# Row sums of reciprocals: a new division of the squaring and summing over four engines, and no batch statistics

## The chip, the cores and the metric

The kernel runs on one NeuronCore of a Trainium2 chip. Its engines are TensorE (PE), VectorE (DVE), ScalarE (ACT), GpSimd (POOL) and SyncE (SP), each with an instruction stream of its own; they meet only at semaphores. SP issues all transfers here, and 16 DMA engines carry them out in the order of issue. The metric is the device time of one execution in microseconds (us), lower being better. A profiled execution has its own time and a span, which goes from the first to the last profiled instruction of the program.

## The reference

```python
x = np.abs(np.random.randn(32, 512, 1024)).astype(np.float32) + 1e-6

def reference(x):
    return np.sum(1.0 / x, axis=-1).astype(np.float32)
```

The input has 67.1 MB and is read once; the output has 64 KB. The kernel divides nowhere: ScalarE computes 1/sqrt(x), and the square of that is 1/x. Each row of 1024 numbers needs three steps then: reciprocal root, square, sum.

## The kernel before

The 16384 rows of x are laid over 128 partitions, 128 rows to each, so that "row u" below is a tile of 128 x 1024 numbers (0.52 MB), one row in every partition. Row 127 is split into two pieces, numbered 127 and 128, of 640 and 384 columns (`PIECES`). The rows go through `ring`, which has 46 places: row u lies at place u modulo 46, so row u can only be loaded when everything that reads row u-46 is done. Results go to `sums`, one column a row.

The order of the work is written out by hand in `PLAN`, a list of tokens. Each engine takes its tokens in this order; a token such as `A35+3` names the operation, the first row and the number of rows, `U59@0` an operation and a buffer. The program adds a semaphore wait wherever a token needs what another engine wrote or still reads. The operations:

- D: a load of so many rows (line 163), always the next ones. SP issues in order, so a load that waits for a place holds up those behind it. There are eight semaphores for the transfers, taken in turn: a transfer also waits until the eighth one before it has landed.
- A: reciprocal root on ScalarE in place (line 170, "Arsqrt"). C: square on ScalarE in place (line 170). Z: square on ScalarE with the sum as a by-product (line 178), followed by a read of the accumulator.
- G: square on GpSimd in place (line 244). T: sum on VectorE (line 247), which follows a C or a G.
- Q: square and sum in one pass on VectorE (line 224), with both inputs the same row of the ring, followed by a read of the accumulator.
- B: two batch-statistics operations on VectorE, one for each half row (line 238). They give count, mean and variance for the even and the odd elements, from which the sum of squares is worked out later. K (lines 258 to 269) does that on GpSimd for rows 0 to 63 and again for rows 64 to 115, five small operations each; M (line 276) adds the outcome to `sums`.
- U, P, L, E, R: another way for 7 of the rows. With a and b the halves of a row, 1/a + 1/b = (a + b)/(ab). TensorE adds the halves into PSUM by products with the identity matrix (U, line 191), GpSimd multiplies them (P, line 184), ScalarE takes reciprocal root and square of the half row ab (L and E, line 201), VectorE multiplies the two and sums (R, line 210).
- O: the early stores of `sums[:, 0:116]`, six of them (line 154); the last twelve columns are stored at the end.

The plan opens with loads of 2, 9, 10, 12 and 13 rows, which fill the ring. Towards the end the loads get short, down to one row, and nearly every row is an A on ScalarE followed by a Q on VectorE. The last tokens are `A117+2 Q116 M0 O0 A119+2 Q117 Q118 A121 Q119 Z120 Q121 A122 A123 Q122 A124 Q123 A125 Q124 A126 Q125 A127 A128 Q127 Z126 Q128`.

Of the kernel before, what the change touches and what calls it, by code (L numbers as in the profile page):

```python
# [11 lines left out]
def kernel(  # L12
# [5 lines left out]
    nc = tc.nc  # L18
    f32 = mybir.dt.float32
    P = 128  # L20
    D = 1024
    H = D // 2
    F = 128
    R = 46
    NP = 5
    PIECES = (640, 384)
    NR = F - sum(PIECES) // D
    KB = (0, 64, 116)
    S = float(2**17)
    FIT = 1.0 - 2.0**-17  # L30

# [2 lines left out]

    PLAN = """
        D2 D9 D10 D12 D13 A0+2 C0 Z1 T0 A2+6 A8 G2 A9 A10 G3+2 T2 C5 C7+2 T5 G6 T8 T3 A11 G9
        A12+3 T4 T6+2 G10 A15 T9 A16+3 A19+2 B17 G18 C11 C12 C13 T10+3 D11 C14 C16 Z15 T13+2 A21  # L40
        A22+5 T16 A27 G19+4 A28+5 Z23 Z24 G25+2 T18+5 D11 Z27 Z31 Z32 G28+3 A33 A34 T25+2 A35+3
        B33 A38+5 G35+3 T28 T29+2 D10 A43+3 Q39 G40 Z34 T35+2 Z38 G42 A46 T37 D7 A47+3 T40 G43
        B41 T42 A50+4 G46 T43 G48 B45 T46 A54 G50 A55+2 B47 T48 G52 Z44 D7 T50 Z49 G56 B51 Z54
        T52 D7 U59@0 A57+2 P59@0 Q53 P60@1 L59 A61+3 B55 U60@1 T56 D4 B57 L60 A64 B58 D4 A65 B61
        A66+2 B62 D2 E59 G66 E60 B64 Z63 R59 K0+64 Z65 D3 R60 T66 U75@2 A68+2 B67 A70 B68 D3
        P75@2 A71 Q69 A72 G71 B70 D2 A73+2 L75 B73 A76+2 T71 A78+2 B74 G76 B77 A80 G79 T76 A81
        B78 A82 A83 T79 A84 B80 E75 Z72 D2 D2 D1 D2 D1 D1 D1 B81 D1 D1 A85 R75 Q82 A86+3 B83 Q85
        A89+3 Q86 B87 Z84 G91 B88 Z89 B90 A92+2 P95@3 U95@3 T91 A94 Q92 L95 Q93 A96 A97 Q94 G96
        U102@4 A98 B97 A99+3 B98 P102@4 T96 L102 B99 G100 E95 U103@5 A104+3 R95 B101 P103@0 T100
        P108@1 L103 A107 B105 U108@6 G106 L108 B107 E102 E103 R102 E108 K64+52 R103 A109+3 T106  # L50
        R108 Z104 Q109 A112 Q110 A113+2 Q111 Q112 A115+2 Q113 Z114 Q115 A117+2 Q116 M0 O0 A119+2
        Q117 Q118 A121 Q119 Z120 Q121 A122 A123 Q122 A124 Q123 A125 Q124 A126 Q125 A127 A128
        Q127 Z126 Q128
    """.split()

    Arsqrt = mybir.ActivationFunctionType.Abs_reciprocal_sqrt
# [19 lines left out]
        tc.tile_pool(name="pspool", bufs=1, space=bass.MemoryType.PSUM)  # L76
    )
    ring = pool.tile([P, R, D], f32)
    stats = pool.tile([P, F, 2, 2, 3], f32)
    part = pool.tile([P, F, 4], f32)  # L80
    total_b = pool.tile([P, F], f32)
    sums = pool.tile([P, F], f32)
    prod = pool.tile([P, NP, H], f32)
    ident = pool.tile([P, P], f32)
    ps = pspool.tile([P, 8, H], f32)
    make_identity(nc, ident)
    nc.gpsimd.memset(stats, 0.0)  # L87
    nc.gpsimd.memset(sums, 0.0)

    def parse(tok):  # L90
        body, _, b = tok[1:].partition("@")
# [3 lines left out]
    def place(u):  # L95
        if u < NR:
            return u, 0, D
        at = sum(PIECES[: u - NR])
        return NR + at // D, at % D, PIECES[u - NR]

    def area(u, n=1):
        r, at, w = place(u)
        return ring[:, r % R : r % R + n, at : at + w]
# [52 lines left out]
    with tc.manual_schedule():  # L156
        for op, u, n, b in (parse(tok) for tok in PLAN):
# [11 lines left out]
            elif op in "AC":  # L169
                inst = nc.scalar.activation(  # L170
                    out=area(u, n),
                    in_=area(u, n),
                    func=Arsqrt if op == "A" else Square,
                    scale=FIT if op == "A" else 1.0,
                )
                note("ACT", inst, writes=rows(u, n))
            elif op == "Z":
                inst = nc.scalar.activation(  # L178
                    out=area(u), in_=area(u), func=Square, accum_out=sums[:, u : u + 1]
                )  # L180
                note("ACT", inst, writes=rows(u))
            elif op == "P":
                slot[u], r = b, u % R
                inst = nc.gpsimd.tensor_tensor(  # L184
                    out=prod[:, b], in0=ring[:, r, :H], in1=ring[:, r, H:], op=mult
                )
                note("POOL", inst, rows(u), [("slot", b)])
            elif op == "U":
                bank[u], r = b, u % R
                for h in range(2):  # L190
                    inst = nc.tensor.matmul(  # L191
                        ps[:, b],
                        lhsT=ident,
                        rhs=ring[:, r, h * H : (h + 1) * H],
                        start=h == 0,
                        stop=h == 1,
                    )
                    note("PE", inst, half(u, h * H), [("bank", b)])
            elif op in "LE":
                pair = prod[:, slot[u]]  # L200
                inst = nc.scalar.activation(  # L201
                    out=pair,
                    in_=pair,
                    func=Arsqrt if op == "L" else Square,
                    scale=S * FIT if op == "L" else 1.0,
                )
                note("ACT", inst, writes=[("slot", slot[u])])
            elif op == "R":
                pair = prod[:, slot[u]]
                inst = nc.vector.tensor_tensor_reduce(  # L210
                    out=pair,
                    in0=pair,
                    in1=ps[:, bank[u]],
                    scale=S,
                    scalar=0.0,
                    op0=mult,
                    op1=add,
                    accum_out=sums[:, u : u + 1],
                )
                note("DVE", inst, [("bank", bank[u])], [("slot", slot[u])])  # L220
            elif op == "Q":
                row, r = area(u), place(u)[0]
                total = sums[:, r : r + 1]
                inst = nc.vector.tensor_tensor_reduce(  # L224
                    out=row,
                    in0=row,
                    in1=row,
                    scale=1.0,
                    scalar=total if r in summed else 0.0,
                    op0=mult,  # L230
                    op1=add,
                    accum_out=total,
                )
                summed.add(r)
                note("DVE", inst, writes=rows(u))
            elif op == "B":
                for h in range(2):
                    inst = nc.vector.bn_stats(  # L238
                        out=stats[:, u, h], in_=ring[:, u % R, h * H : (h + 1) * H]
                    )  # L240
                    note("DVE", inst, reads=half(u, h * H))
            elif op == "G":
                row = area(u, n)
                inst = nc.gpsimd.tensor_tensor(out=row, in0=row, in1=row, op=mult)  # L244
                note("POOL", inst, writes=rows(u, n))
            elif op == "T":
                inst = nc.vector.tensor_reduce(  # L247
                    out=sums[:, u : u + n],
                    in_=area(u, n),
                    axis=mybir.AxisListType.X,  # L250
                    op=add,
                )
                note("DVE", inst, reads=rows(u, n))
            elif op == "K":
                mean = stats[:, u : u + n, :, :, 1].rearrange("p f h e -> p (f h e)")
                var = stats[:, u : u + n, :, :, 2].rearrange("p f h e -> p (f h e)")
                flat = part[:, u : u + n].rearrange("p f q -> p (f q)")
                nc.gpsimd.tensor_tensor(out=flat, in0=mean, in1=mean, op=mult)  # L258
                nc.gpsimd.tensor_scalar(  # L259
                    out=flat, in0=flat, scalar1=float(H // 2), scalar2=None, op0=mult  # L260
                )
                nc.gpsimd.tensor_tensor(out=flat, in0=flat, in1=var, op=add)  # L262
                nc.gpsimd.tensor_tensor(  # L263
                    out=part[:, u : u + n, :2],
                    in0=part[:, u : u + n, :2],
                    in1=part[:, u : u + n, 2:],
                    op=add,
                )
                nc.gpsimd.tensor_tensor(  # L269
                    out=total_b[:, u : u + n],  # L270
                    in0=part[:, u : u + n, 0],
                    in1=part[:, u : u + n, 1],
                    op=add,
                )
            elif op == "M":
                nc.gpsimd.tensor_tensor(  # L276
                    out=sums[:, : KB[-1]],
                    in0=sums[:, : KB[-1]],
                    in1=total_b[:, : KB[-1]],
                    op=add,  # L280
                )
            elif op == "O":
                for c in range(0, KB[-1], 20):
                    store(c, min(c + 20, KB[-1]))
        store(KB[-1], F)


# [28 lines left out]
```

## Time and profile before

| | |
|---|---|
| median of 3 runs | 167.15 us (166.9 to 167.3) |
| the profiled execution's own time | 166.88 us |
| its span | 165.0 us |
| busy: ACT, DVE, POOL, PE | 149.0, 122.1, 85.2, 20.5 us |
| load queue, share of 16 DMA engines' span | 95.9% |
| read from HBM | 67.11 MB, 407 GB/s over the span |

The page of the profile gives the busy time of each engine, the DMA queues, the chain of waits that ended last and the costliest groups of instructions. "Lnnn" is a line of the kernel. A group's line gives the tiles, the shape, the count, the busy time in us and the mean duration in ns, and then the idle time of the engine ahead of it and what ended that. A line of the timeline gives start and duration in us, engine, line, operation, tiles and shapes, and the number of merged instructions. A table by stretches gives, for each stretch, the busy time of PE, PEld, DVE, ACT and POOL with their instruction counts, the granted clock of TensorE, the busy share of the DMA engines and GB/s; a share counts whole packets where they end or begin and can so pass 1. In the lines on DMA issues stand the size in KB and the time from issue to landing, and SPq is the issuing queue.

### The profile page before, as it was taken

The page shows a single profiled execution, that of the slowest core. Times are in us where ns is not written, and L with a number is a line of the kernel's source. Part 1 is how long each engine was busy: PE and PEld are TensorE (multiplying, and loading weights), DVE is VectorE, ACT ScalarE, POOL GpSimd, SP SyncE. Part 2 cuts the span into 40 slices and gives each one's busy share as a digit, 9 for nine tenths or more (in the row PEclk, how much of TensorE's full clock was granted, in tenths as well). Part 3 has the DMA queues.
Part 4 walks back from the last instruction along what each step waited for, and adds up shares of the span by engine and source line. Part 5 has one row for each costly group of instructions (what it writes and reads, how often), then busy time and mean ns, then how long its engine had stood idle before and what let it go on. Part 6 is the DMA issues. An engine that isn't in the chain of part 4 may idle for free.

```text
span 165.0 us, 529 instructions
## 1 busy us (share of the span) xinstructions
PE 20.5 (12%) x28; PEld 7.0 (4%) x28; DVE 122.1 (74%) x161; ACT 149.0 (90%) x131; POOL 85.2 (52%) x52
## 2 busy tenths in 40 slices
PE   0000000000000000000019026000009764000000
PEld 0000000000000000000013011000002211000000
DVE  0020027954920499999999999899998999999992
ACT  3630997999999999999999999999999999999992
POOL 5000069922019999999996088380043889403000
PEclk9999999999999999999999965555555589955555
DMA  5999989899999998989998999999999999999960
GB/s 183 500 429 445 447 367 489 381 500 453 413 413 413 413 524 349 513 362 470 404 453 367 467 381 440 445 438 417 424 408 429 433 414 426 423 423 421 404 204 2
DMA packets 4754, 67.19 MB, mean 407 GB/s; under 512 B 1424, under 2 KB 1552, under 8 KB 2192
## 3 DMA queue, kind: packets, MB, share of 16 engines
q1 hardware_dynamic: 4752, 67.18, 95.9%
q14 instruction: 2, 0.02, 0.0%
HBM read 67.11 MB, written 0.07 MB: 407 GB/s over the span
## 4 chain that ended last, share of the span: by engine, by line
ACT 43%; DMA 39%; DVE 14%; issue 1%; SPq 1%; DVEq 0%
DMA ring<-in_x_dram 39%; ACT ring L170 35%; DVE sums L247 7%; ACT ring L178 6%; DVE ring L224 4%; DVE stats L238 3%; ACT prod L201 3%; SPq L163 1%; DVE sums L224 0%; DVEq L224 0%; DVEq L311 0%
## 5 line engine op out<-in xcount | busy, mean ns | idle before, releaser
L170 ACT ACTIVATE ring<-ring 128x1024 f32<-128x1024 f32 (+4 forms) x74 | 120.0, 1688 | 12.1 <-DMA ring<-in_x_dram 12.0
L244 POOL TENSOR_TENSOR ring<-ring 128x1024 f32<-128x1024 f32 (+3 forms) x26 | 66.5, 2581 | 56.7 <-ACT ring L170 56.7
L247 DVE TENSOR_REDUCE sums<-ring 128x1 f32<-128x1024 f32 (+3 forms) x33 | 50.6, 1563 | 35.9 <-POOL ring L244 23.4
L238 DVE BATCH_NORM_STATS2 stats<-ring 128x6 f32<-128x512 f32 x62 | 38.7, 677 | 2.5 <-ACT ring L170 2.5
L191 PE MATMUL ps<-ring,ident 128*128 128x512 f32 x28 | 20.5, 878 | 117.8 <-POOL ring L244 86.0
L224 DVE CUSTOM_DVE_ANT_0 ring<-ring 128x1024 f32<-128x1024 f32 (+1 forms) x25 | 30.8, 1281 | 1.5 <-ACT ring L170 1.3
L178 ACT ACTIVATE ring<-ring 128x1024 f32<-128x1024 f32 x21 | 21.8, 1040 | 0.0
L191 PEld LDWEIGHTS ps<-ring,ident 128*128 128x128 f32 x28 | 7.0, 272 | 130.4 <-POOL ring L244 86.0
L184 POOL TENSOR_TENSOR prod<-ring 128x512 f32<-128x512 f32 x7 | 9.9, 1420 | 0.6 <-DMA ring<-in_x_dram 0.5
L201 ACT ACTIVATE prod<-prod 128x512 f32<-128x512 f32 x14 | 8.1, 615 | 0.0
L276 POOL TENSOR_TENSOR sums<-sums,total_b 128x116 f32<-128x116 f32 x1 | 1.3, 1256 | 7.4 <-DVE sums L224 7.4
L210 DVE CUSTOM_DVE_ANT_0 prod<-prod,ps 128x512 f32<-128x512 f32 x7 | 4.6, 674 | 0.0
L178 ACT ACTIVATION_READ_ACCUMULATOR ring<-ring 128x1 f32 x21 | 3.9, 187 | 0.0
L224 DVE DVE_READ_ACCUMULATOR2_ANT sums<- 128x1 f32 x26 | 2.1, 82 | 0.0
L65 ACT ACT_TABLE_LOAD x1 | 1.3, 1283 | 0.7 <-PEq L300 0.7
L259 POOL TENSOR_SCALAR part<-part 128x256 f32<-128x256 f32 (+1 forms) x2 | 1.6, 792 | 0.2
L262 POOL TENSOR_TENSOR part<-part,stats 128x256 f32<-128x256 f32 (+1 forms) x2 | 1.5, 748 | 0.2
L87 POOL MEMSET stats<- 128x1536 f32 x1 | 1.4, 1378 | 0.0
L258 POOL TENSOR_TENSOR part<-stats 128x256 f32<-128x256 f32 (+1 forms) x2 | 1.2, 596 | 0.0
L263 POOL TENSOR_TENSOR part<-part 128x128 f32<-128x128 f32 (+1 forms) x2 | 0.8, 381 | 0.2
L224 DVE CUSTOM_DVE_ANT_0 ring<-ring,sums 128x384 f32<-128x384 f32 x1 | 0.6, 618 | 0.1
L269 POOL TENSOR_TENSOR total_b<-part 128x64 f32<-128x64 f32 (+1 forms) x2 | 0.6, 296 | 0.2
(8 smaller groups left out, 1.7 us busy)
## 6 DMA issues: line engine op xcount, KB each, us to landing
ring<-in_x_dram SPq DMA_DIRECT2D x2, 5632.0 KB, 26.7
ring<-in_x_dram SPq DMA_DIRECT2D x3, 3584.0 KB, 32.4
ring<-in_x_dram SPq DMA_DIRECT2D x2, 5120.0 KB, 28.4
ring<-in_x_dram SPq DMA_DIRECT2D x1, 6656.0 KB, 56.1
ring<-in_x_dram SPq DMA_DIRECT2D x6, 1024.0 KB, 30.1
ring<-in_x_dram SPq DMA_DIRECT2D x1, 6144.0 KB, 41.1
ring<-in_x_dram SPq DMA_DIRECT2D x1, 4608.0 KB, 15.4
ring<-in_x_dram SPq DMA_DIRECT2D x2, 2048.0 KB, 39.4
```

The source lines that it names most:

```text
L163: inst = nc.sync.dma_start(out=area(u, m), in_=x_v[:, r : r + m, at : at + w])
L170: inst = nc.scalar.activation(out=area(u, n), in_=area(u, n), func=Arsqrt if op == "A" else Square, scale=FIT if op == "A" else 1.0,)
L178: inst = nc.scalar.activation(out=area(u), in_=area(u), func=Square, accum_out=sums[:, u : u + 1])
L184: inst = nc.gpsimd.tensor_tensor(out=prod[:, b], in0=ring[:, r, :H], in1=ring[:, r, H:], op=mult)
L191: inst = nc.tensor.matmul(ps[:, b], lhsT=ident, rhs=ring[:, r, h * H : (h + 1) * H], start=h == 0, stop=h == 1,)
L201: inst = nc.scalar.activation(out=pair, in_=pair, func=Arsqrt if op == "L" else Square, scale=S * FIT if op == "L" else 1.0,)
L210: inst = nc.vector.tensor_tensor_reduce(out=pair, in0=pair, in1=ps[:, bank[u]], scale=S, scalar=0.0, op0=mult, op1=add, accum_out=sums[:, ...
L224: inst = nc.vector.tensor_tensor_reduce(out=row, in0=row, in1=row, scale=1.0, scalar=total if r in summed else 0.0, op0=mult, op1=add, acc ...
L238: inst = nc.vector.bn_stats(out=stats[:, u, h], in_=ring[:, u % R, h * H : (h + 1) * H])
L244: inst = nc.gpsimd.tensor_tensor(out=row, in0=row, in1=row, op=mult)
L247: inst = nc.vector.tensor_reduce(out=sums[:, u : u + n], in_=area(u, n), axis=mybir.AxisListType.X, op=add,)
L259: nc.gpsimd.tensor_scalar(out=flat, in0=flat, scalar1=float(H // 2), scalar2=None, op0=mult)
```

## The change

The plan is rewritten, and B, K and M leave it, with the tiles `stats`, `part` and `total_b` and two memsets on GpSimd. By token, before and after:

| token | before: tokens (rows) | after: tokens (rows) |
|---|---|---|
| D | 26 | 28 |
| A | 66 (122) | 74 (124) |
| C | 8 (9) | 5 (5) |
| Z | 21 | 24 |
| G | 26 (35) | 29 (35) |
| T | 33 (44) | 24 (39) |
| Q | 26 | 60 |
| B | 31 | 0 |
| V | 0 | 1 |
| U, P, L, E, R | 7 each | 5 each |
| early stores | 6 | 3 |

Counts of A and Q include the two pieces of row 127. V is new: a VectorE operation that multiplies one row by 1, adds 0 and sums on the way. It stands in place of a T for row 2, which GpSimd squared. The pieces of row 127 have 512 columns each. The plan opens with loads of 2, 9, 9, 10, 6 and 10 rows. The rows of U, P, L, E, R are 28, 71, 92, 101 and 105.

```diff
-    PIECES = (640, 384)
+    PIECES = (512, 512)
     NR = F - sum(PIECES) // D
-    KB = (0, 64, 116)
+    DONE = 116
+    PART = 39
...
     PLAN = """
...
+        D2 D9 D9 D10 D6 D10 A0 A1 Q0 Z1 A2+5 A7+3 G2 G4+3 V2 A10 Z3 Z7 Z8 A11 G9 T4 A12+2 T5 G10
+        A14 T6 D7 A15 G12 T9+2 A16+2 G13 A18+2 Q15 Z14 G18 Z17 T13 Z19 Q16 C11 P28@0 U28@0 A20+2
+        T11+2 D9 A22+4 G20+2 T18 A26 Q23 G24 A27 T20+2 L28 A29 G25 A30+2 A32 G26 A33+3 G29 Z32
+        G30+2 T29 Z33 E28 C22 R28 C27 T22 G34 T24+4 D9 A36+2 G35 A38+2 G36+2 T30+2 D8 A40+2
+        A42+2 G39 T34+4 A44+2 G41 A46 G42 A47+6 Q43 G44 T41+2 G45 T44 Z40 Q48 Z46 G49+2 Z47 T45
+        Z51 C38 A53 T38+2 D7 D6 G52 A54+2 T49+2 D5 G53 A56+4 Q54 G55 T52+2 A60+2 G56 T55 D5 Z58
+        Q57 C59 G60 A62 T56 A63+2 T59 G61 A65+2 Q62 A67+3 G65 T60+2 D5 A70 Q64 Z63 D4 T65 Z67
+        P71@1 U71@1 Q66 D3 A72 L71 A73 Q69 A74+2 Q70 Q73 A76+2 Q74 A78 Q75 Z68 D3 Q76 A79 Q77
+        A80+2 Q78 A82+2 Q79 Q80 A84+2 Q81 Z72 D2 D2 D1 D1 D1 D1 D1 D1 D1 D1 Q82 A86+2 Q83 Q84
+        A88 Q85 A89+3 Q87 Q88 Z86 P92@2 U92@2 Q89 A93+4 Q90 Q91 L92 Z93 Q94 E71 Q95 E92 P101@3
+        U101@3 A97 R71 A98+3 R92 Q96 Q97 L101 Q98 Z100 Q99 E101 P105@4 U105@4 A102 R101 A103+2
+        Q102 L105 Q103 A106 Q104 E105 A107 R105 A108 Q106 A109+2 Q107 Q108 A111 Q110 A112 A113
+        Q111 Z109 Q112 A114 Q113 A115 Q114 A116 Q115 O0 A117 Q116 A118 A119 Q117 A120 Q118 A121
+        Q119 A122 Q120 Z121 Q122 A123 A124 Q123 A125 Q124 A126 Q125 A127 A128 Q127 Z126 Q128
     """.split()
...
-    nc.gpsimd.memset(stats, 0.0)
-    nc.gpsimd.memset(sums, 0.0)
...
+            elif op == "V":
+                inst = nc.vector.tensor_scalar(
+                    out=area(u),
+                    in0=area(u),
+                    scalar1=1.0,
+                    scalar2=0.0,
+                    op0=mult,
+                    op1=add,
+                    accum_out=sums[:, u : u + 1],
+                )
+                note("DVE", inst, writes=rows(u))
             elif op == "O":
-                for c in range(0, KB[-1], 20):
-                    store(c, min(c + 20, KB[-1]))
-        store(KB[-1], F)
+                for c in range(0, DONE, PART):
+                    store(c, min(c + PART, DONE))
+        store(DONE, F)
```

More of the change, by code (lines that the diff above doesn't have):

```diff
@@ L38 @@
     PLAN = """
[L39 to L50, printed above, removed]
@@ L51 @@
-        R108 Z104 Q109 A112 Q110 A113+2 Q111 Q112 A115+2 Q113 Z114 Q115 A117+2 Q116 M0 O0 A119+2
-        Q117 Q118 A121 Q119 Z120 Q121 A122 A123 Q122 A124 Q123 A125 Q124 A126 Q125 A127 A128
-        Q127 Z126 Q128
+        D2 D9 D9 D10 D6 D10 A0 A1 Q0 Z1 A2+5 A7+3 G2 G4+3 V2 A10 Z3 Z7 Z8 A11 G9 T4 A12+2 T5 G10
+        A14 T6 D7 A15 G12 T9+2 A16+2 G13 A18+2 Q15 Z14 G18 Z17 T13 Z19 Q16 C11 P28@0 U28@0 A20+2
+        T11+2 D9 A22+4 G20+2 T18 A26 Q23 G24 A27 T20+2 L28 A29 G25 A30+2 A32 G26 A33+3 G29 Z32
@@ L78 @@
     ring = pool.tile([P, R, D], f32)
-    stats = pool.tile([P, F, 2, 2, 3], f32)
-    part = pool.tile([P, F, 4], f32)
-    total_b = pool.tile([P, F], f32)
     sums = pool.tile([P, F], f32)
@@ L221 @@
             elif op == "Q":
-                row, r = area(u), place(u)[0]
+                r, at, _ = place(u)
+                _, last, w = place(u + n - 1)
+                row = ring[:, r % R, at : last + w]
                 total = sums[:, r : r + 1]
@@ L234 @@
                 summed.add(r)
[L235 to L241, printed above, removed]
+                note("DVE", inst, writes=rows(u, n))
             elif op == "G":
@@ L253 @@
                 note("DVE", inst, reads=rows(u, n))
[L254 to L260, printed above, removed]
-                )
[L262 to L281, printed above, removed]
+            elif op == "V":
[7 more added lines that the diff above has]
+                    accum_out=sums[:, u : u + 1],
+                )
+                note("DVE", inst, writes=rows(u))
             elif op == "O":
-                for c in range(0, KB[-1], 20):
-                    store(c, min(c + 20, KB[-1]))
-        store(KB[-1], F)
+                for c in range(0, DONE, PART):
+                    store(c, min(c + PART, DONE))
+        store(DONE, F)
 _INS = ['x']
```

## The prediction

> **What bounds the kernel now.** I read the page first: span, engines, queues.
>
> ```profile
> span 165.0 us, 529 instructions
> ...
> PE 20.5 (12%) x28; PEld 7.0 (4%) x28; DVE 122.1 (74%) x161; ACT 149.0 (90%) x131; POOL 85.2 (52%) x52
> ...
> q1 hardware_dynamic: 4752, 67.18, 95.9%
> q14 instruction: 2, 0.02, 0.0%
> ...
> ACT 43%; DMA 39%; DVE 14%; issue 1%; SPq 1%; DVEq 0%
> ```
>
> The load queue (95.9%) is busier than any engine. Next, the busy time by stretches: from 2.5 us to 155 us the DMA share (next to last column) stays at 0.98 to 1.02, while ACT, DVE and POOL vary.
>
> ```profile
> 2.50:20.00 17.50, 0.00 (x0) 0.00 (x0) 1.22 (x1) 7.44 (x5) 0.21 (x2) 1.00 1.02 435
> 80.00:100.00 20.00, 7.13 (x11) 3.03 (x12) 20.00 (x31) 20.00 (x24) 13.79 (x11) 0.90 0.98 419
> 140.00:155.00 15.00, 0.00 (x0) 0.00 (x0) 14.31 (x28) 15.00 (x15) 3.39 (x6) 0.62 1.01 416
> 160.00:161.00 1.00, 0.00 (x0) 0.00 (x0) 1.00 (x3) 1.00 (x3) 0.00 (x0) 0.50 0.00 0
> ```
>
> So x streams in without a gap and compute only has to keep up. The chain of waits (last line of the first fence) puts only 39% on the DMA, since ACT is nearly as long a path through the same time; what counts is when the last bytes land and who ends after them. From the DMA issues, windowed around the end (issue time; KB and us to landing):
>
> ```profile
> 143.66 0.33 SPq L163 DMA_DIRECT2D ring<-in_x_dram  x1
> ring<-in_x_dram SPq DMA_DIRECT2D x1, 512.0 KB, 15.0
> 148.58 0.33 SPq L163 DMA_DIRECT2D ring<-in_x_dram  x1
> ring<-in_x_dram SPq DMA_DIRECT2D x1, 192.0 KB, 11.5
> 162.21 0.33 SPq L154 DMA_DIRECT2D out_dram<-sums  x1
> out_dram<-sums SPq DMA_DIRECT2D x1, 6.0 KB, 1.4
> ```
>
> Row 126 lands at 158.7, the last piece at 160.1, the last store is issued at 162.21 and lands at 163.6; the span ends at 165.0. The 2.1 us between last landing and last store are DVE's, from the timeline:
>
> ```profile
> 151.08 1.91 ACT L170 ACTIVATE ring<-ring 128x2048 f32<-128x2048 f32 x1
> 154.88 1.04 ACT L170 ACTIVATE ring<-ring 128x1024 f32<-128x1024 f32 x1
> 155.95 1.23 DVE L224 CUSTOM_DVE_ANT_0 ring<-ring 128x1024 f32<-128x1024 f32 x1
> 160.54 0.82 DVE L224 CUSTOM_DVE_ANT_0 ring<-ring 128x640 f32<-128x640 f32 x1
> 161.52 0.62 DVE L224 CUSTOM_DVE_ANT_0 ring<-ring,sums 128x384 f32<-128x384 f32 x1
> ```
>
> Row 122's Arsqrt ends at 155.92; its square-and-sum Q starts at 155.95 and from there DVE has no real pause: four Q in 4.59 us, 1.15 each, then the two pieces.
>
> **The change part by part.** Prices are steps of the chain of waits (start, us, what); they are a little shorter than the durations, as neighbours overlap.
>
> ```profile
> 80.23 1.12 DVE sums L247
> 133.87 2.66 ACT ring L170
> 137.04 0.95 ACT ring L170
> 137.99 2.08 ACT prod L201 x4
> 143.75 4.55 ACT ring L170 x3
> 148.30 1.04 ACT ring L178 x2
> ```
>
> Arsqrt (A) costs 0.95 for one row, (4.55-0.95)/2 = 1.80 for two, 2.66 for three; Z (square with sum, and its read) 1.04; L or E 0.52; T (sum of a row) 1.12. From the groups kept apart by form come the longer ones: A of five rows 4.45 less the 0.09 by which one row's 1.04 exceeds its step of 0.95, so 4.36; A of four, between three and five, 3.51; T of two rows 2.28 - 0.08 = 2.20, where 0.08 is the same overlap on DVE (a Q takes 1.23 and steps by 1.15).
>
> ```profile
> L170 ACT ACTIVATE ring<-ring 128x5120 f32<-128x5120 f32 x3 | 13.4, 4452 | 0.0
> L247 DVE TENSOR_REDUCE sums<-ring 128x2 f32<-128x2048 f32 x5 | 11.4, 2276 | 0.0
> L238 DVE BATCH_NORM_STATS2 stats<-ring 128x6 f32<-128x512 f32 x62 | 38.7, 677 | 2.5 <-ACT ring L170 2.5
> ```
>
> *Transfers.* The same bytes come in 28 transfers instead of 26. What a cut costs, from the first matmuls that wait for a landing:
>
> ```profile
> 128.88 3.78 PE L191 MATMUL ps<-ring,ident 128*128 128x512 f32 x4 [1.12 <-DMA ring<-in_x_dram]
> 133.77 1.98 PE L191 MATMUL ps<-ring,ident 128*128 128x512 f32 x4 [1.11 <-DMA ring<-in_x_dram]
> 136.25 1.12 PE L191 MATMUL ps<-ring,ident 128*128 128x512 f32 x2 [0.50 <-DMA ring<-in_x_dram]
> ```
>
> Four rows took 4.89 us, two rows 2.48: 2 x 2.48 - 4.89 = 0.07 a transfer, about 1.21 a row. Two more: +0.14, last landing 160.2 (bounds 0 and 0.2, nothing in the trace lets a cut gain).
>
> *Does the queue run dry?* The tightest issue in the changed list is the D9 of rows 62 to 70, which reuses the places of rows 16 to 24 and waits for T24+4. That T waits for C27, so for ACT, which works without a pause from the landing of rows 2 to 10:
>
> ```profile
> 16.56 5.32 ACT L170 ACTIVATE ring<-ring 128x6144 f32<-128x6144 f32 x1 [6.85 <-DMA ring<-in_x_dram]
> 61.51 0.33 SPq L163 DMA_DIRECT2D ring<-in_x_dram  x1
> ```
>
> From A2+5 to C27: 11 single A or C 10.45, five pairs 9.0, two triples 5.32, a four 3.51, a five 4.36, eight Z 8.32, L and E 1.04, together 42.0, to 58.6 (rows 11 to 19 land at 16.56 + 9 x 1.21 + 0.07 = 27.5, just ahead of A11, which comes up at 27.7; later rows have more time). Then DVE: T22 1.12 and T24+4 about 4.4, to 63.2 (before, a D11 went out at 61.51). The 46 rows on their way land at 59.0; 16 rows more, already issued, add 16 x 1.21 + 0.14, so data last until 78.5. That is 15 us early; the later loads come out 17 us early or more by the same adding, and the single-row ones, held until the eighth transfer before has landed, still have seven rows, 9 us, in flight. The load stream stays whole.
>
> *Statistics to Q.* 31 B (two of 677 ns, 1.2 together) go, 34 more Q at 1.15 come, and T rows fall from 44 to 39; L, E and R go from 7 rows to 5. So 37.2 + 5.6 + 1.2 go and 39.1 + 1.15 come: DVE gets some 4 us less to do. The one V (multiply with sum) has no row; T (1.12) and Q (1.15) are nearest, I take 1.15, and twice that would be hidden, since DVE idles for data there.
>
> *Collisions with POOL.* Q reads the ring twice, and where one meets a POOL multiplication it stops:
>
> ```profile
> 64.74 8.14 POOL L244 TENSOR_TENSOR ring<-ring 128x3072 f32<-128x3072 f32 x2
> 68.31 2.83 DVE L224 CUSTOM_DVE_ANT_0 ring<-ring 128x1024 f32<-128x1024 f32 x1
> 72.85 1.89 POOL L244 TENSOR_TENSOR ring<-ring 128x1024 f32<-128x1024 f32 x1
> 101.32 1.49 DVE L224 CUSTOM_DVE_ANT_0 ring<-ring 128x1024 f32<-128x1024 f32 x1
> 102.06 2.50 POOL L244 TENSOR_TENSOR ring<-ring 128x1024 f32<-128x1024 f32 x1 [0.33 <-ACT ring L170]
> ```
>
> Undisturbed, Q takes about 1.23 and one row of G 1.89; here Q took 2.83 and 1.49, G 2.50. The Trainium skill, page "SBUF — State Buffer", section "Who interferes with whom", says that a VectorE instruction with two SBUF inputs and a GpSimd one that reads SBUF lock each other out for the whole instruction, first come first served; the trace agrees (2.83). By that rule ten meetings cost DVE anything from nothing to 10 x 1.89 = 18.9 us.
>
> Is there room? After T24+4 (63.2) DVE has, up to Q120: six T of two rows 13.2, one of four 4.4, six single 6.7, 50 Q 57.5, four R (half a row, 0.61) 2.4: 84.2, to 147.4. Q122 must start by 155.9 (tail, below): 8.5 us of room. Q43, Q48, Q54, Q57, Q62, Q64 stand among G, and four P among the late Q, so ten meetings. The two rows cost DVE 1.6 and 0.3, mean 0.94; POOL, coming second, pays about half of them: 4.7, bounds 0 and 9.4. I take 4.7: DVE still waits for data. Q15, Q16 and Q23 fall where T24+4 waits for C27 anyway.
>
> *POOL.* The two memsets at the start and the 11 operations on the statistics go. They filled time in which POOL had no rows to square (it is busy 52% of the span), and only the six early stores waited for them. Nothing; were the cover gone, the early stores would go out later, and the last one need not wait for them.
>
> *Stores.* Three early ones instead of six. They queue behind the loads already issued, and the last store, issued 2.1 us after the last landing, takes only 1.4 us: none of the six stood in its way. Nothing.
>
> *Tail.* Rows 119 and 120 end with the 20th transfer, before with the 19th: ACT starts them at 151.08 + 0.07 = 151.15. A119, A120, A121, A122 3.80, Z121 1.04, A123 starts at 155.99 and ends at 157.03 (rows 121 to 123 have landed by then, 1.28 apart). Q123 starts at 157.06, three Q 3.45, to 160.51. Q127 and Q128 now have 512 columns, between the 0.82 and 0.62 of 640 and 384: 0.72 each, with the 0.16 that Q128 waited for the sum of Q127: 162.11. Arsqrt of the last piece (0.52 + 0.09, as an L of half a row) ends at 160.9, in time. Before it was 162.14. Sum: 165.0, and 166.88 for the profiled execution as before; the median of the runs lies 0.27 above it, so 167.15, rounded with the 0.03 gained to **167.1 us**.
>
> **The rivals.**
> 1. *DVE is late (slower).* Place: the Q between Q64 and Q122. It decides from 8.5 us of extra DVE time; beyond that every us shows at the end. All ten meetings at 0.94 are 9.4, and a Q that costs 0.01 more is 0.5 over 50. I price it at 1 us late: 168.1. Against it: DVE has 4 us less work.
> 2. *Fewer instruction packets (faster).* The q14 row shows two packets of 8 KB during the run. In the window from 73.0 us that packet is
>
> ```profile
> q14 instruction: 1, 0.01, 4.8%
> ```
>
> of 16 engines x 0.4 us, so 0.31 us on one of the 16, and a load waits for its slowest one. Without one the end is 0.31 earlier, without both 0.62: 166.8 or 166.5. For it: POOL falls from 52 busy instructions to 40, PE from 28 to 20. Against it: the longest programs do not shrink (ACT 131 to 138, DVE 161 to 155). The Trainium skill, page "Runtime: NRT & Kernel Launch", section "Instruction fetch mechanics", has fetches in blocks of 16 KiB as a program runs on; here two packets make 0.02 MB together, 8 KB each.
> 3. *The tail is shorter (faster).* If DVE keeps up better, only the last piece counts, its Arsqrt and its Q: 160.2 + 0.61 + 0.72 = 161.6, 0.5 earlier: 166.6. Against it: Z121 in front of A123 is the same step as Z120 before.
> 4. *A load comes late (slower).* It needs 15 us at T24+4: 168 or more.
>
> **How the numbers follow.** Chances: forecast 0.44, DVE late 0.25, fewer packets 0.18, shorter tail 0.10, late load 0.03. The range takes in both packets gone (166.5) and DVE a little over a us late: 166.4 to 168.3; the forecast's own is 166.8 to 167.4. Within 0.2% (0.33 us, about what a measurement here can tell) 0.44, faster 0.28, slower 0.28.
>
> **What would show it.** Right: a DMA share near 1 from 2.5 to 155 us, the last landing at 160.2, no wait of ACT for a load over 1 us after 17 us, Q near G of up to 3 us with no later effect, DVE idle a few times between 115 and 150, Q123 right behind Arsqrt of row 123. Wrong: a last landing under 159.9, a q14 row with fewer packets, DVE without a pause from 95 us on with Q starting well after their Arsqrt, or a DMA share that dips near 78 us.

## The result, and the profile after

The changed kernel takes 166.56 us (median of 9 runs, 166.34 to 166.96) against 167.02 us for the kernel before in the same comparison (9 runs, 166.73 to 167.30): a ratio of 0.9974, 95% interval 0.9963 to 0.9985. It is 0.26% faster, about 0.43 us. The forecast was 167.1 us and no change; the measured time lies within its range (166.4 to 168.3), a little outside the 0.2% that was to count as no change. The profiled execution took 166.41 us with a span of 164.2 us (before: 166.88 and 165.0).

From the page of the changed kernel, the lines that answer to the first fence of the prediction:

```profile
span 164.2 us, 505 instructions
...
PE 18.5 (11%) x20; PEld 5.9 (4%) x20; DVE 122.9 (75%) x156; ACT 149.0 (91%) x138; POOL 77.1 (47%) x40
...
q1 hardware_dynamic: 4608, 67.18, 96.2%
q14 instruction: 2, 0.02, 0.0%
...
DMA 50%; ACT 42%; DVE 5%; issue 1%; SPq 0%; DVEq 0%
```

ACT is busy for the same 149.0 us, and there are still two instruction packets. DVE is not relieved: 122.9 us instead of 122.1. The stretches show that the loads stream as before (next to last column, the DMA share):

```profile
2.50:20.00 17.50, 0.00 (x0) 0.00 (x0) 1.23 (x2) 6.65 (x5) 0.00 (x0) 1.00 1.04 446
40.00:60.00 20.00, 3.41 (x4) 0.80 (x3) 11.13 (x10) 19.56 (x17) 19.00 (x9) 1.00 0.99 427
80.00:100.00 20.00, 0.77 (x1) 0.50 (x2) 20.00 (x19) 19.89 (x17) 14.36 (x8) 1.00 1.00 433
140.00:155.00 15.00, 0.00 (x0) 0.00 (x0) 15.00 (x27) 15.00 (x17) 0.00 (x0) 0.51 1.00 414
```

Now the end, from the timeline and the DMA issues, windowed (issue time; KB and us to landing):

```profile
150.97 0.33 SPq L157 DMA_DIRECT2D ring<-in_x_dram  x1
ring<-in_x_dram SPq DMA_DIRECT2D x1, 256.0 KB, 9.0
156.90 1.23 DVE L220 CUSTOM_DVE_ANT_0 ring<-ring 128x1024 f32<-128x1024 f32 x1
160.34 0.69 DVE L220 CUSTOM_DVE_ANT_0 ring<-ring 128x512 f32<-128x512 f32 x1
161.18 0.75 DVE L220 CUSTOM_DVE_ANT_0 ring<-ring,sums 128x512 f32<-128x512 f32 x1
162.00 0.33 SPq L148 DMA_DIRECT2D out_dram<-sums  x1
out_dram<-sums SPq DMA_DIRECT2D x1, 6.0 KB, 1.4
```

The last piece lands at 160.0 (before 160.1), Q123 starts at 156.90, the last store goes out at 162.00 (before 162.21) and lands at 163.4 (before 163.6). That is 0.2 us. The span, however, is shorter by 0.77: 1.41 us passed before between the landing of the last store and the end of the span, and 0.83 us now. More than half of the difference is behind everything that the prediction looked at.

Two things happen there. SP waits for the semaphores of the transfers, one after the other; then GpSimd leads a barrier (a point that every engine must reach before any goes on). The semaphore instructions of SP (SPq) and GpSimd (POOLq), each line from the view of the closing line of the program in a narrow window (count, shortest/median/longest in ns, first and last start). Before, SP in 163.62 to 163.85 us, just behind the landing, and POOL in 163.93 to 164.38:

```profile
L311 SPq EVENT_SEMAPHORE  x4: 28/28/931, 162.7 to 163.8; - x4
L311 POOLq EVENT_SEMAPHORE  x2: 17/17/17, 163.9 to 164.4; - x2
```

After, SP in 163.41 to 163.48 and POOL in 163.57 to 163.66:

```profile
L284 SPq EVENT_SEMAPHORE  x1: 28/28/28, 163.4 to 163.4; - x1
L284 POOLq EVENT_SEMAPHORE  x2: 17/17/17, 163.6 to 163.7; - x2
```

Before, the wait that ends with the last store (931 ns long) has three more behind it, up to 163.8; after, it is the last wait. And GpSimd stood still for 0.41 us between its first two semaphore instructions of the barrier (163.96 to 164.37 in the records), where it now needs 0.06.

### The profile page after: what moved, and what is told of

It is laid out like the page before. It is cut to its first block, busy times and chain, and to the rows that moved or that the text cites. A ratio compares the mean times of both kernels' runs of the same rounds, so it can differ in the third digit from the quotient of the medians.

```text
span 164.2 us, 505 instructions
## 1 busy us (share of the span) xinstructions
PE 18.5 (11%) x20; PEld 5.9 (4%) x20; DVE 122.9 (75%) x156; ACT 149.0 (91%) x138; POOL 77.1 (47%) x40
## 4 chain that ended last, share of the span: by engine, by line
DMA 50%; ACT 42%; DVE 5%; issue 1%; SPq 0%; DVEq 0%
DMA ring<-in_x_dram 50%; ACT ring L164 34%; ACT ring L172 7%; DVE sums L237 3%; DVE ring L220 2%; ACT prod L195 1%; SPq L157 0%; DVE sums L220 0%; DVEq L220 0%; DVEq L284 0%
## 5 line engine op out<-in xcount | busy, mean ns | idle before, releaser
L164 ACT ACTIVATE ring<-ring 128x1024 f32<-128x1024 f32 (+6 forms) x79 | 118.8, 1571 | 11.9 <-DMA ring<-in_x_dram 11.7
L220 DVE CUSTOM_DVE_ANT_0 ring<-ring 128x1024 f32<-128x1024 f32 (+1 forms) x59 | 74.8, 1317 | 9.7 <-ACT ring L164 9.5
L234 POOL TENSOR_TENSOR ring<-ring 128x1024 f32<-128x1024 f32 (+2 forms) x29 | 68.8, 2407 | 23.6 <-ACT ring L164 23.6
L237 DVE TENSOR_REDUCE sums<-ring 128x1 f32<-128x1024 f32 (+2 forms) x24 | 44.3, 1878 | 12.4 <-POOL ring L234 9.4
L185 PE MATMUL ps<-ring,ident 128*128 128x512 f32 x20 | 18.5, 1079 | 118.7 <-DMA ring<-in_x_dram 118.7
L172 ACT ACTIVATE ring<-ring 128x1024 f32<-128x1024 f32 x24 | 25.0, 1041 | 0.0
L178 POOL TENSOR_TENSOR prod<-ring 128x512 f32<-128x512 f32 x5 | 7.5, 1507 | 34.0 <-DMA ring<-in_x_dram 34.0
L195 ACT ACTIVATE prod<-prod 128x512 f32<-128x512 f32 x10 | 6.1, 615 | 0.2 <-POOL prod L178 0.2
L220 DVE DVE_READ_ACCUMULATOR2_ANT sums<- 128x1 f32 x60 | 4.8, 80 | 0.0
L204 DVE CUSTOM_DVE_ANT_0 prod<-prod,ps 128x512 f32<-128x512 f32 x5 | 3.3, 682 | 1.6 <-ACT prod L195 1.6
L204 DVE DVE_READ_ACCUMULATOR2_ANT sums<- 128x1 f32 x5 | 0.4, 81 | 0.0
```

Of the source, the lines that this page charges most:

```text
L164: inst = nc.scalar.activation(out=area(u, n), in_=area(u, n), func=Arsqrt if op == "A" else Square, scale=FIT if op == "A" else 1.0,)
L172: inst = nc.scalar.activation(out=area(u), in_=area(u), func=Square, accum_out=sums[:, u : u + 1])
L178: inst = nc.gpsimd.tensor_tensor(out=prod[:, b], in0=ring[:, r, :H], in1=ring[:, r, H:], op=mult)
L185: inst = nc.tensor.matmul(ps[:, b], lhsT=ident, rhs=ring[:, r, h * H : (h + 1) * H], start=h == 0, stop=h == 1,)
L195: inst = nc.scalar.activation(out=pair, in_=pair, func=Arsqrt if op == "L" else Square, scale=S * FIT if op == "L" else 1.0,)
L204: inst = nc.vector.tensor_tensor_reduce(out=pair, in0=pair, in1=ps[:, bank[u]], scale=S, scalar=0.0, op0=mult, op1=add, accum_out=sums[:, ...
```

## The experiments

Theory A: the gain is behind the last store. With 33 transfers the last one stands on a semaphore that SP waits for third of six; with 32 on the last. And GpSimd stops at a fixed place of its program, which the shorter program moved out of the closing barrier, to behind the span: the time outside the span (time less span) grew from 1.91 to 2.16 us (medians). Theory B, the rival: the gain lies in the tail on DVE and in the loads. The kernels of one comparison ran on one chip beside the kernel before. There the spread of the times was wider than in the first comparison: 166.7 to 168.3 us for the kernel before. So for the small terms the trace is the sharper witness.

**33 transfers again.** Four early stores of 29 columns.

```diff
-    PART = 39
+    PART = 29
```

> The changed kernel with four early stores of 29 columns in place of three of 39: 33 transfers in all, as before the change. Theory A (a part of the gain lies behind the last store: SP waits at the end for the semaphores of the transfers one after the other, in a fixed order, and with 33 transfers the last store is not the last of these waits): the waits after its landing come back, 0.2 us between landing and SP's first drain, so the span grows by about 0.2 us and the ratio to the kernel before goes from 0.9974 to about 0.9986. Theory B (the gain is the tail on VectorE and the loads): an early store lies beside the loads, ratio unchanged at 0.9974. Theory C (stores cost DMA time): last landing later by under 0.05 us, ratio under 0.9980.

Measured: ratio 0.9988 (0.9967 to 1.0009). The three waits are back behind the landing at 163.88, SP in 163.89 to 164.10, and GpSimd has no stop:

```profile
L284 SPq EVENT_SEMAPHORE  x4: 28/28/927, 163.0 to 164.1; - x4
L284 POOLq EVENT_SEMAPHORE  x2: 17/17/17, 164.2 to 164.3; - x2
```

From landing to the end of the span 1.00 us, that is 0.17 more. The ratio agrees with A but its interval holds all theories; the trace tells them apart.

**A GpSimd program as long as before.** 14 one-column memsets at its start.

```diff
     make_identity(nc, ident)
+    spare = pool.tile([P, 1], f32)
+    for _ in range(14):
+        nc.gpsimd.memset(spare, 0.0)
```

> The changed kernel with 14 one-column memsets on GpSimd ahead of everything else, so that its GpSimd program is as long as before the change; GpSimd is idle there until 21 us. Theory A (at the end GpSimd stood still for 0.4 us between two semaphore instructions of the closing barrier, because of where its program had got to; the shorter program moved that out of the span): the stop of 0.4 us between these two instructions comes back, the span grows by about 0.35 us, and the time outside the span shrinks from 2.17 towards 1.88 us, so the ratio to before is between 0.9974 and 0.9995. Theory B (tail and loads): no stop, span and ratio as for the changed kernel, 164.2 to 164.5 us and 0.9974.

Measured: ratio 0.9991 (0.9976 to 1.0005). The stop is back (window 165.18 to 165.63; this profiled execution was 1.4 us longer in its loads), from landing to the end 1.24 us, and the time outside the span is 1.92 us again:

```profile
L287 POOLq EVENT_SEMAPHORE  x2: 17/17/17, 165.2 to 165.6; - x2
```

**The place moved further.** 30 memsets as shown, and in a later comparison 15.

```diff
+    spare = pool.tile([P, 1], f32)
+    for _ in range(30):
+        nc.gpsimd.memset(spare, 0.0)
```

> The same with 30 memsets, so that the place of the program at which GpSimd stood still comes up among its row products long before the end. Theory A with a stop at a fixed place of the program: the stop falls where GpSimd has nothing urgent to do, neither the closing barrier nor the time after the span shows it, and the kernel is about 0.3 us faster than the changed one, ratio about 0.9956. Theory A2 (the stop hangs on the time or on the barrier, not on the place in the program): as for 14 memsets. Theory B: 0.9974.

> The changed kernel with 15 one-column memsets on GpSimd ahead of everything else, one more than in the run with 14. Theory A with a stop at a fixed place of the program: the place moves one instruction forward, to the first semaphore instruction of GpSimd's closing barrier, at which GpSimd waits for SP from 135 us on anyway; so no stop of 0.4 us between the first and the second in the trace, time outside the span 1.9 us as with 14, and faster than the changed kernel by about 0.25 us, ratio 0.996, unless the third instruction packet that it then fetches during the loads (0.31 us on one of 16 DMA engines) holds up the last landing, ratio then 0.9974. Theory A2 (stop belongs to the barrier): stop still there, span 0.35 us longer than the changed kernel's.

Measured: 0.9976 (0.9960 to 0.9992) with 30, and 0.9966 (0.9937 to 0.9995) with 15. One memset more than 14, and the stop is gone from the barrier. So the stop belongs to a place in the program, not to the barrier or to a time. First line with 30, second with 15:

```profile
L287 POOLq EVENT_SEMAPHORE  x2: 17/17/17, 163.7 to 163.8; - x2
```

```profile
L287 POOLq EVENT_SEMAPHORE  x2: 17/17/17, 164.1 to 164.2; - x2
q14 instruction: 3, 0.02, 0.0%
```

With 15 the third instruction packet falls at 139.8 us, with 30 at 79.0, while GpSimd waits or works in the middle: it comes when GpSimd passes that place. So the stop and an instruction fetch belong together. But GpSimd does not stand still for that packet: in the four kernels with the stop in the barrier the next instruction packet begins 0.69 to 0.71 us after the stop has ended (before: stop up to 164.37, packet at 165.06 in the records), and none moves during it. What GpSimd waits for stays open. The time outside the span is 2.04 us with 15 memsets and 1.98 with 30. Neither run is the clear gain over the changed kernel that theory A hoped for (0.9956 and 0.996): 0.9966 and the changed kernel's 0.9974 cannot be told apart.

**32 transfers in the kernel before.** Five early stores of 24 columns.

```diff
-                for c in range(0, KB[-1], 20):
-                    store(c, min(c + 20, KB[-1]))
+                for c in range(0, KB[-1], 24):
+                    store(c, min(c + 24, KB[-1]))
```

> The kernel before with five early stores of 24 columns instead of six of 20: 32 transfers. Theory A: the last store is the last of SP's closing waits, about 0.2 us saved behind its landing, ratio about 0.9988 and a span of about 164.8 us. Theory B: 1.000.

Measured: 0.9990 (0.9974 to 1.0006). In the trace one wait is left behind the landing, GpSimd's stop stays, and from landing to the end it is 1.22 us instead of 1.41:

```profile
L311 SPq EVENT_SEMAPHORE  x1: 28/28/28, 163.9 to 163.9; - x1
L311 POOLq EVENT_SEMAPHORE  x2: 17/17/17, 164.1 to 164.5; - x2
```

**Both in the kernel before, and both undone in the changed one.** The first is the last kernel with one memset of one column on GpSimd at the start; the statistics stay. The second is the changed kernel with four early stores and 14 memsets.

> The kernel before, its statistics and its plan untouched, with five early stores of 24 columns (32 transfers) and one memset of one column on GpSimd at the start, which moves GpSimd's stop one instruction forward, out of the closing barrier. Theory A (nearly all of the gain is behind the last store and owes nothing to the statistics): 0.19 us less in SP's closing waits, 0.35 us less in GpSimd's part of the closing barrier, 0.1 us more outside the span; ratio 0.9974, the whole gain of the change. Rival (the gain is the new division of the work, in the loads or on VectorE): ratio 1.000.

> The changed kernel with both ends undone: four early stores (33 transfers) and 14 one-column memsets on GpSimd at the start. Theory A: 0.19 us come back in SP's closing waits, 0.35 us in GpSimd's part of the closing barrier, 0.25 us less outside the span; ratio between 0.9991 and 1.000, the change without its end is worth at most 0.15 us. Rival: ratio 0.9974.

Measured: the kernel before with the new end 0.9972 (0.9955 to 0.9990), the changed kernel with the old end 1.0025 (1.0007 to 1.0044). The two ends, kernel before first:

```profile
L314 SPq EVENT_SEMAPHORE  x1: 28/28/28, 164.3 to 164.3; - x1
L314 POOLq EVENT_SEMAPHORE  x2: 17/17/17, 164.5 to 164.6; - x2
```

```profile
L287 SPq EVENT_SEMAPHORE  x4: 28/28/922, 163.7 to 164.8; - x4
L287 POOLq EVENT_SEMAPHORE  x2: 17/17/17, 165.0 to 165.4; - x2
```

This settles where the gain lies: one store less and one memset more give the kernel before the whole gain, with every B, K and M in place. The second value lies above the 0.9991 to 1.000 that theory A gave it: without its end the change is a little slower than the kernel before, by 0.1 to 0.4%. The two transfers more may account for some 0.15 us of that (below); the rest is open, and the changed kernel itself was not run beside it on that chip. Outside the span theory A missed as well: 1.91 us for the first, where 0.1 more was expected, and 1.98 for the second, 0.19 less than in the changed kernel where 0.25 was expected.

From the records, the time from the landing of the last store to the end of the span, in us:

| kernel | transfers | GpSimd's stop in the barrier | landing to end |
|---|---|---|---|
| before | 33 | yes | 1.41 |
| before, five early stores | 32 | yes | 1.22 |
| before, the same and one memset | 32 | no | 0.84 |
| after | 32 | no | 0.83 |
| after, four early stores | 33 | no | 1.00 |
| after, 14 memsets | 32 | yes | 1.24 |
| after, both | 33 | yes | 1.39 |
| after, 15 or 30 memsets | 32 | no | 0.84, 0.83 |

The two terms add up: 0.15 to 0.19 for the 33rd transfer, 0.38 to 0.41 for the stop. The records also give the place: in all four kernels with the stop in the barrier it stands just ahead of GpSimd's 69th recorded instruction. With one memset or 15 the 69th is the first of the barrier, at which GpSimd waits anyway; the changed kernel has only 60.

**The changed kernel once more.**

> The changed kernel once more, beside the next three runs on the same chip. Theory A (of some 0.43 us gained, about 0.2 us are SP's closing waits, 0.1 us are GpSimd's stop moved behind the span, the rest is in the tail on VectorE and below 0.15 us): ratio 0.9974 again, time outside the span 2.16 us.

Measured: 0.9981 (0.9959 to 1.0004), time outside the span 2.18 us; beside it the kernel before had 1.90.

**How much room DVE has.** Rival 1 of the prediction turned on this. Three, and then eight, extra sums of row 66 on DVE ahead of Q66.

```diff
-        P71@1 U71@1 Q66 D3 A72 ...
+        P71@1 U71@1 X66 X66 X66 Q66 D3 A72 ...
...
+    spare = pool.tile([P, 1], f32)
...
+            elif op == "X":
+                inst = nc.vector.tensor_reduce(
+                    out=spare, in_=area(u), axis=mybir.AxisListType.X, op=add
+                )
+                note("DVE", inst, reads=rows(u))
```

> The changed kernel with three more sums over row 66 on VectorE ahead of Q66, into a spare column: 3 x 1.12 = 3.4 us of extra VectorE time in the stretch that the prediction's rival 1 is about. By the prediction's sum VectorE has 8.5 us of room there, less the 4.4 us that the trace shows for the meetings with GpSimd, so 4.1 us: the 3.4 us are absorbed, time as for the changed kernel within 0.2 us. The rival (VectorE is the bound in this stretch): the end moves by the full 3.4 us.

> The same with eight more sums, 9.0 us of extra VectorE time. By the prediction's sum 4.1 us are absorbed and the rest shows: 4.9 us slower than the changed kernel, VectorE without a pause up to the last Q. If the room were the whole 8.5 us: 0.5 us slower. If there were none: 9.0 us slower.

Measured: ratios 1.0149 (1.0110 to 1.0188) and 1.0550 (1.0501 to 1.0598); medians 170.0 and 176.5 us beside 166.96 for the changed kernel, so 3.0 and 9.6 us more, each known to some 0.7 to 0.8 us. I expected 4.1 us of room. The group of Q on DVE from 98.6 us on, after; then from 99 us on with three sums more; then the sums of the run with eight (busy us, mean ns, idle us):

```profile
L220 DVE CUSTOM_DVE_ANT_0 ring<-ring 128x1024 f32<-128x1024 f32 (+1 forms) x49 | 58.8, 1258 | 1.3 <-ACT ring L164 1.1
```

```profile
L221 DVE CUSTOM_DVE_ANT_0 ring<-ring 128x1024 f32<-128x1024 f32 (+1 forms) x49 | 59.1, 1270 | 0.0
L246 DVE TENSOR_REDUCE spare<-ring 128x1 f32<-128x1024 f32 x3 | 3.6, 1215 | 0.1
```

```profile
L246 DVE TENSOR_REDUCE spare<-ring 128x1 f32<-128x1024 f32 x8 | 9.7, 1218 | 0.2
```

The extra sums take 3.7 and 9.9 us with their pauses, more than the 3.4 and 9.0 that I had put, as each waits for the one before it. All but 0.7 and 0.3 us of that shows in the time. In the changed kernel DVE idles 1.3 us in these 63 us; with three sums more the idle time is gone. The sums also moved the later Q against the GpSimd products: three were held to 2.3 us, where the changed kernel has two at 2.3 and one at 1.55, and that used up 0.7 of the 1.3 us. So DVE is at most about 1.3 us away from being the bound.

## Why the prediction was right, and where it was not

*Loads.* Right. 28 transfers, a share of 0.99 to 1.04 in each stretch shown. From the first landing to the last the records of the two profiled executions give 154.42 us before and 154.58 after: +0.16, where the step gave +0.14 for two transfers. That it agrees to 0.02 is luck: the other profiles give 154.8 and 155.1 us with the plan of before and 154.5 to 156.0 with the new one. ACT never waited for a load for more than 0.44 us after 17 us. Two instruction packets before and after: rival 2 did not occur. The tight load went out when the sum said (63.2), and its data lasted until 78.6 (the loads before it landed then in the records; the sum said 78.5):

```profile
63.20 0.33 SPq L157 DMA_DIRECT2D ring<-in_x_dram  x1
ring<-in_x_dram SPq DMA_DIRECT2D x1, 4608.0 KB, 26.3
```

*Collisions.* Right in mechanism, and in the sum. Of the Q beside GpSimd products the costliest were held to 2.3 us. Here are two of them, and the GpSimd product that the first one met:

```profile
99.32 1.58 POOL L178 TENSOR_TENSOR prod<-ring 128x512 f32<-128x512 f32 x1 [3.19 <-DMA ring<-in_x_dram]
99.71 2.28 DVE L220 CUSTOM_DVE_ANT_0 ring<-ring 128x1024 f32<-128x1024 f32 x1
122.18 2.29 DVE L220 CUSTOM_DVE_ANT_0 ring<-ring 128x1024 f32<-128x1024 f32 x1
```

All collisions after 63 us cost DVE 4.4 us in the records (Q43, Q48, Q54, Q57, Q69, Q90, Q102), where 4.7 were taken. That the sums are so near is partly luck: ten meetings at 0.47 us were taken, and it was seven at 0.63. The product at 99.32 ends at 100.90, and the Q that began in its midst ends 1.1 us later. These lines agree with the rule that the prediction took from the Trainium skill, page "SBUF — State Buffer", section "Who interferes with whom": one of the two waits for the whole instruction of the other.

*Statistics to Q, and DVE's room.* The step "DVE gets some 4 us less to do" held for the work and not for the time: the collisions took it back (122.9 us busy against 122.1; 116.6 against 120.2 without what the collisions cost, by the records). And the step "8.5 us of room" was mis-sized. It counted from T24+4 to Q122. The collisions took 4.4 us of it, as the step allowed for, but it also took in a wait that DVE has from 77.1 us on, where T38+2 needs ScalarE:

```profile
79.38 2.29 DVE L237 TENSOR_REDUCE sums<-ring 128x2 f32<-128x2048 f32 x1 [2.25 <-ACT ring L164]
```

Time lost there cannot be spent later. The room that counts for the end, from Q66 on, is 1.3 us. The forecast held because even with its collisions DVE kept those 1.3 us; rival 1 had the right place, but was nearer than the text made it: after the collisions it decides from some 1.3 us of extra time behind Q66, not from 4.1.

*POOL and stores.* This is the step that failed. "Nothing", said of both, is right for all that lies ahead of the last store, and the sum then took over the 2.9 us between Q128 and the end of the span from the kernel before as if they were a constant. They are not: in that time SP goes through its waits and GpSimd through the barrier, and the first depends on the number of transfers, the second on the length of GpSimd's program. 0.19 us for the 33rd transfer, and for the stop 0.38 less in the span and 0.25 more outside it (that this is the stop's is inferred): together 0.32 of the 0.43 us, the rest not assigned. Both terms were in the trace of before: a semaphore instruction of SP of 931 ns with three behind it, and 0.41 us between two neighbours on GpSimd. I read the span's end as one number.

*Tail.* Right to 0.2 us. The sum had Q123 at 157.06 and Q128's end at 162.11; measured 156.90 and 161.93, and the first landing was 0.25 us earlier in this execution. From the last landing to the last store it is 2.02 us after and 2.13 before, but over the kernels that share a plan (those with extra sums left aside) 2.02 to 2.20 after and 2.13 to 2.20 before, so the change of the tail is below what I can tell. Q of 512 columns took 0.69 and 0.75 (0.72 taken).

*The time.* 165.0 for the span was 0.8 too high. The 0.27 us that I put between the profiled execution and the median was 0.15 after (166.56 against 166.41). The time came out within the range because the term that was missing is small. It lies on the faster side, to which the prediction gave 0.28, but by neither of the two rivals named for it: the packets stayed, and the tail did not measurably shorten.

## What to carry to other kernels

When the sum of a change comes out at nothing, cost the closing of the program too: what the issuing engine still waits for behind its last store, and whether any engine stops in the closing barrier. Both depend on counts (transfers, instructions) that an edit changes without meaning to, and here they outweighed 31 replaced operations. And room on an engine is only what it idles behind the last point that can make it late; idle time ahead of a wait that stays is no room.

## What the runs showed of the hardware that was not expected

- GpSimd stops 0.39 to 0.41 us at a fixed place of its program when nothing covers it. One instruction more in front moves the stop to another instruction. Where the place lies in the middle of the kernel, a third instruction packet shows in the queue (three in all with 15 or 30 memsets), and the stop costs nothing that can be seen. The Trainium skill, page "Runtime: NRT & Kernel Launch", section "Instruction fetch mechanics", calls the cost of crossing a block of the program mostly hidden. If the stop is such a crossing, which no run here shows, that agrees with the runs where the place lies in the middle, and not with the 0.41 us in the closing barrier.
- With the stop out of the barrier and the program too short to reach its place within the span, the time outside the span went from 1.91 to 2.16 us. That GpSimd stops there, behind the span, is inferred from this time alone; no record shows it. In the two runs with extra sums on DVE it was 2.6 to 2.7 us, which I cannot explain.
- The third load, nine rows, takes from 10.9 to 12.6 us (from the landing before it to its own) in the profiles of the changed kernel and its variants. All the loads together took 154.5 to 156.0 us in the same profiles, a spread wider than what the change gained, and only partly in step with the third load (11.95 us there went with 154.6 in all in the run with 33 transfers). What sets it stays open.
